# Keeping split weights in DRAM for later chunks

## The chip, the core and the metric

One Trainium2 chip, of which the kernel uses one core. The metric is the device time of one execution in microseconds (us). [...]

## The reference

One layer of a decoder with four kinds of token mixers side by side, over 2048 tokens of width 1024, and an MLP of width 4096 behind them. The shapes that matter here: w_in has 1024 rows and 3852 columns, w_out is 1024 x 1024.

```python
h = _modulate(x, norm_mix_gain[l], shift1, scale1)
z = (h @ w_in[l]).astype(jnp.float32)
(hq, hf, hi, hg, dq, dk, dv, fq, fk, fv, fg, ff, mq, mk, mv, mo, mi, mf) = _split(z, IN_WIDTHS)
y_a = _hgrn2(hq, hf, hi, hg, ...)            # gated linear recurrence
y_b = _diff_attention(dq, dk, dv, ...)       # two score maps, mixed
y_c = _forgetting_attention(fq, fk, fv, fg, ff, ...)
y_d = _mlstm(mq, mk, mv, mo, mi, mf, ...)    # matrix memory recurrence
y = jnp.concatenate([y_a, y_b, y_c, y_d], axis=-1) @ w_out[l]
x = x + (gate1[:, None, :] * y).astype(x.dtype)
h = _modulate(x, norm_ff_gain[l], shift2, scale2)
y = jnp.square(jax.nn.relu(h @ w_ff1[l])) @ w_ff2[l]
x = x + (gate2[:, None, :] * y).astype(x.dtype)
```

## The kernel before

The tokens are worked in four chunks of 512. The mixing part is written as two strands whose steps are woven into each other. Strand a is attention: for each chunk the forgetting attention (fox_attn), then the differential attention (diff_attn). Strand b first makes queries, keys and values of all four chunks (seven loads of weights a chunk), and then, chunk by chunk, the dense products and the serial parts of the two recurrences (mlstm, hgrn), each in two halves; as soon as attention has finished a chunk, the output projection of that chunk follows (w_out_dense), and then the second norm. After the mixing part comes the MLP.

The order of the instructions on each engine is not the written one: a scheduler plans it before the run, from priorities and from a simulation of its own. Each engine, and the queue of SP, from which almost all DMAs are issued, then works its list in that order: one that waits holds all that stand behind it.

Weights come in by load_w (L199). It takes the next of two tiles for the high part (whi, 128 x 8 x 268) and the next of two for the low part (wlo). The 1024 rows of a load go in pieces through four raw buffers: for 256 columns four pieces of 256 rows. For a piece, SP issues the DMA of the raw weights (L208; two DMAs where the columns come from two places, as in win2, L948), ACT rounds it into the high part (L194), and POOL subtracts the high part from the raw piece, which gives the low part (L197). So a raw buffer is free again when POOL is done with it, and a weight tile when the last matmul that reads it is done. A load is used by dense_cm (L509 to L511, 24 matmuls for 128 output columns with all 512 tokens) or by dense_tm (L521 to L523, 24 matmuls for 128 tokens), once for all tokens of the chunk.

A chunk's recurrences make nine loads: four for mlstm (L1003, L1016, for both halves), and for hgrn two with two pieces of columns (L1130), two of 128 columns (L1138) and one of 256 (L1145). Its output projection makes four (L1307). The same weights are loaded and split again for each of the four chunks.

What else the prediction names: L679 are the score matmuls, L686 is DVE's eviction of scores with a running minimum, L695 is ACT's exponential, L881 is DVE's mixing of the two score maps of the differential attention, L734 are the transposes behind it, L737 (ACT) and L738 (DVE) split a transposed map into its parts, L748 are the products with the values. L647 and L660 load keys, queries and values for attention from DRAM. L1211 to L1215 are levels of hgrn. L243 and L249 are ada: the modulation vector is made block by block on DVE from w_ada; 16 of its blocks, each with four loads of 256 KB through two buffers, are spread over the serial parts of the recurrences of the first two chunks.

Of the kernel before, what the change touches and what calls it, by code (L numbers as in the profile page):

```python
# [9 lines left out]
F32 = mybir.dt.float32  # L10
# [60 lines left out]
def hybrid_block(ctx: ExitStack, tc: tile.TileContext, a: dict, out: bass.AP, dbg: dict):  # L71
# [124 lines left out]
            nc.vector.tensor_copy(h, r)  # L196
        nc.gpsimd.tensor_tensor(l, r, f32(h), ALU.subtract)  # L197

    def load_w(pieces, n, stage=raws):  # L199

        h, l = ring(whi), ring(wlo)
        step = stage[0].shape[1] // n
        for k0 in range(0, KT, step):
            ks = slice(k0, k0 + step)
            r = ring(stage)[:, :step * n].rearrange("p (k n) -> p k n", k=step)
            for c0, src in pieces:
                w = src.shape[-1]
                nc.sync.dma_start(r[:, :, c0:c0 + w], src[k0 * P:(k0 + step) * P].rearrange("(k p) n -> p k n", p=P))  # L208
            split_w(r, h[:, ks, :n], l[:, ks, :n])
        return h, l  # L210

    w_in = a["w_in"][0]
# [263 lines left out]
    if True:  # L476
# [469 lines left out]
            return pc  # L946

        def win2(c0, c1):  # L948
            return load_w([(0, w_in[:, c0:c0 + P]), (P, w_in[:, c1:c1 + P])], G)


        gates_of = {}
# [176 lines left out]
        def hgrn_dense(c, j, st):  # L1129
            W = win2(O_HF + j * P, O_HQ + j * P)  # L1130
            st["fq"] = []
            for blk in range(2):
                o = dense_cm(W, blk)
                st["fq"].append(FB.get())
                with soon("b"):
                    nc.scalar.activation(FB[st["fq"][blk]][:, :CT], o, AF.Copy)
                yield
            o = dense_cm(win(O_HG + j * P, P), 0)  # L1138
            st["g"] = FB.get()
            with soon("b"):  # L1140
                nc.vector.tensor_copy(FB[st["g"]][:, :CT], o)
            yield

            if j == 0:
                W = win(O_HI)  # L1145
                hval[c] = (FB.get(), FB.get())
                for tb in range(TB):
                    o = dense_tm(W, tb, G)
                    with soon("b"):
                        nc.scalar.activation(tok(hval[c][0], P)[:, tb], o[:, :P], AF.Copy)  # L1150
                        nc.vector.tensor_copy(tok(hval[c][1], P)[:, tb], o[:, P:G])
                    yield
# [134 lines left out]
        def w_out_dense(c, st, u):  # L1287
# [16 lines left out]
                t0 = c * CT + tb * P  # L1304
                nc.sync.dma_start(FB[xs[tb]][:, :512], a["x"][0, t0:t0 + P, u * 512:(u + 1) * 512])
            for n in range(2):
                W = load_w([(0, a["w_out"][0][:, u * 512 + n * G:u * 512 + (n + 1) * G])], G)  # L1307
                ns = slice(n * G, (n + 1) * G)
                for tb in range(TB):
                    o = dense_tm(W, tb, G, st["h"])  # L1310
# [506 lines left out]
```

## Time and profile before

| | us |
|---|---|
| median of 3 runs | 3220.86 |
| lowest, highest | 3217.7, 3223.13 |
| the profiled execution | 3222.74 |
| its span, first to last instruction | 3221.0 |
| busy in the span: TensorE, DVE, ACT, POOL | 2973.0, 2053.9, 1650.5, 777.6 |
| granted clock, mean | 0.945 |

Times in the rows below are counted from the start of the span of the profiled execution. A group of instructions is given by its line in the kernel, its engine, its operation and the names of what it writes and reads, with the number of instructions behind the x. Busy time of an engine is the union of its instructions; matmuls are pipelined, so a busy TensorE is not TensorE at its peak. The granted clock is the share of full speed that TensorE had.

### The profile page before, as it was taken

The numbers are of one execution on the slowest core, as the hardware profiler recorded it, in microseconds if no ns is written. First come the engines' busy times: TensorE is split into PE (matmuls) and PEld (weight loads), VectorE is DVE, ScalarE is ACT, GpSimd is POOL, SyncE is SP. The second block draws the span as 40 slices with busy tenths as digits, with TensorE's granted clock in tenths as the row PEclk, the third lists the DMA queues.
The fourth block names the chain that finished last, engine by engine and source line by source line (L and its number), as shares of the span: only waits on it lengthen the run. The fifth ranks groups of instructions, "written<-read, shape, count | busy, mean of one in ns | idle before, by whom it ended". The sixth has DMA issues, their size and how long they took to land.

```text
span 3221.0 us, 50522 instructions
## 1 busy us (share of the span) xinstructions
PE 2973.0 (92%) x17398; PEld 2494.0 (77%) x17398; DVE 2053.9 (64%) x4642; ACT 1650.5 (51%) x3576; POOL 777.6 (24%) x800
## 2 busy tenths in 40 slices
PE   5989999899888899999988679999999999999999
PEld 3878989678667688887777467888788778887887
DVE  4377567767768867766778638666866545445553
ACT  2566667556545556556555536555555533332331
POOL 3454344334334344444344120000000000000000
PEclk8999999889889799999989789999999999999999
DMA  6876766535434364545343345555555577566662
GB/s 230 267 238 213 243 219 206 186 113 172 125 105 149 117 199 116 163 135 173 92 144 117 100 150 169 152 149 155 172 157 152 167 235 238 183 194 214 222 205 76
DMA packets 506565, 548.70 MB, mean 170 GB/s; under 512 B 41401, under 2 KB 352788, under 8 KB 504260
## 3 DMA queue, kind: packets, MB, share of 16 engines
q1 hardware_dynamic: 504004, 541.28, 53.4%
q10 hardware_dynamic: 2304, 4.20, 0.4%
q8 instruction: 137, 2.24, 0.3%
q14 instruction: 120, 0.98, 0.1%
HBM read 385.83 MB, written 159.51 MB: 169 GB/s over the span
## 4 chain that ended last, share of the span: by engine, by line
PE 53%; DVE 13%; DMA 6%; ACT 3%; issue 2%; POOL 1%; SPq 0%; DVEq 0%; POOLq 0%; ACTq 0%
PE bank L1560 6%; PE bank L1561 6%; PE bank L1559 5%; PE bank L1782 5%; PE bank L1781 5%; PE bank L1780 5%; PE bank L142 3%; PE bank L521 2%; PE bank L748 2%; PE bank L523 2%; PE bank L522 2%; PE bank L679 2%; PE bank L734 2%; DMA stage<-in_w_ff 2%; DVE FA L881 2%
## 5 line engine op out<-in xcount | busy, mean ns | idle before, releaser
L197 POOL TENSOR_TENSOR wlo<-raw,whi 128x512 fp32r<-128x512 f32 (+1 forms) x304 | 408.7, 1364 | 387.1 <-ACT whi L194 346.0
L521 PE MATMUL bank<-whi,AH 128*128 128x256 f32 (+1 forms) x1536 | 452.3, 295 | 25.1 <-ACT whi L194 11.1
L522 PE MATMUL bank<-wlo,AH 128*128 128x256 f32 (+1 forms) x1536 | 445.7, 290 | 0.9 <-POOL wlo L197 0.9
L523 PE MATMUL bank<-whi,AH 128*128 128x256 f32 (+1 forms) x1536 | 444.8, 290 | 0.0
L695 ACT ACTIVATE FA<-FA,att_m 128x512 f32<-128x512 f32 (+3 forms) x480 | 310.5, 650 | 153.4 <-DVE att_m L692 146.2
L686 DVE TENSOR_SCALAR_CACHE_REDUCE FA<-bank 128x512 f32<-128x512 f32 (+3 forms) x480 | 284.3, 603 | 69.6 <-PE bank L679 40.0
L521 PEld LDWEIGHTS bank<-whi,AH 128*128 128x128 f32 x1536 | 299.1, 195 | 35.9 <-ACT whi L194 11.4
L522 PEld LDWEIGHTS bank<-wlo,AH 128*128 128x128 f32 x1536 | 299.4, 195 | 3.8 <-POOL wlo L197 1.4
L523 PEld LDWEIGHTS bank<-whi,AH 128*128 128x128 f32 x1536 | 298.4, 195 | 2.7 <-issue 1.9
L679 PE MATMUL bank<-AL 97*128 97x512 f32 (+10 forms) x640 | 241.9, 436 | 57.1 <-DVE FA L686 53.8
L748 PE MATMUL bank<-TS,AL 128*128 128x256 f32 (+1 forms) x1152 | 238.4, 314 | 15.7 <-DVE TS L738 7.2
L194 ACT ACTIVATE whi<-raw 128x512 fp32r<-128x512 f32 (+1 forms) x304 | 186.5, 628 | 114.9 <-PE bank L523 45.0
L737 ACT ACTIVATE TS<-bank 128x512 fp32r<-128x512 f32 (+1 forms) x288 | 158.8, 569 | 135.0 <-PE bank L734 118.5
L738 DVE TENSOR_TENSOR TS<-bank,TS 128x512 fp32r<-128x512 f32 (+1 forms) x288 | 185.7, 654 | 63.3 <-ACT TS L737 60.2
L734 PE MATMUL bank<-ident,FA 128*128 128x128 f32 x1088 | 198.9, 292 | 24.9 <-DVE FA L881 24.0
L748 PEld LDWEIGHTS bank<-TS,AL 128*128 128x128 f32 x1152 | 186.5, 203 | 35.8 <-DVE TS L738 11.6
L679 PEld LDWEIGHTS bank<-AL 97*128 97x128 f32 (+2 forms) x640 | 122.1, 208 | 94.5 <-DVE FA L686 78.6
L734 PEld LDWEIGHTS bank<-ident,FA 128*128 128x128 f32 x1088 | 139.7, 150 | 38.5 <-DVE FA L881 28.5
L509 PE MATMUL bank<-AH,whi 128*128 128x512 f32 x384 | 159.1, 419 | 7.1 <-DVE FB L1107 2.1
L510 PE MATMUL bank<-AH,whi 128*128 128x512 f32 x384 | 159.0, 414 | 2.5 <-DMA AH<-hl 2.5
L511 PE MATMUL bank<-AH,wlo 128*128 128x512 f32 x384 | 157.9, 411 | 0.0
L881 DVE SCALAR_TENSOR_TENSOR FA<-FA,att_ro,FA 128x512 f32<-128x512 f32 (+3 forms) x160 | 128.2, 848 | 1.2
(908 smaller groups left out, 7478.2 us busy)
## 6 DMA issues: line engine op xcount, KB each, us to landing
r<-tmp SPq DMA_DIRECT2D x224, 256.0 KB
raw<-in_w_in SPq DMA_DIRECT2D x144, 256.0 KB
stage<-r SPq DMA_DIRECT2D x139, 256.0 KB
stage<-in_w_ff SPq DMA_DIRECT2D x32, 1024.0 KB
stage<-in_w_ff SPq DMA_DIRECT2D x107, 256.0 KB
raw<-in_w_in SPq DMA_DIRECT2D x192, 128.0 KB
tmp<-r SPq DMA_DIRECT2D x85, 256.0 KB
AL<-kD SPq DMA_DIRECT2D x80, 224.0 KB
```

The lines of the kernel that those rows point to most:

```text
L197: nc.gpsimd.tensor_tensor(l, r, f32(h), ALU.subtract)
L521: nc.tensor.matmul(o[:, :n], hTh[:, k, t], h[:, k, :n], start=(k == 0), stop=False)
L522: nc.tensor.matmul(o[:, :n], hTh[:, k, t], l[:, k, :n], start=False, stop=False)
L523: nc.tensor.matmul(o[:, :n], hTl[:, k, t], h[:, k, :n], start=False, stop=(k == KT - 1))
L679: nc.tensor.matmul(o[:, :w], lh, rh(p)[:, :w], start=(i == 0), stop=(i == len(mm) - 1 and not diag))
L686: nc.vector.tensor_scalar(FA[e][:, :w], o[:, :w], -1.0, 3.0e38, ALU.mult, ALU.min, accum_out=st[:, p:p + 1])
L695: nc.scalar.activation(FA[e][:, :w], FA[e][:, :w], AF.Exp, scale=-1.0, bias=mx, accum_out=sz[:, p:p + 1] if n > 1 else z)
L734: nc.tensor.transpose(o[:, c0:c0 + P], FA[e][:, (sb % 4) * P:(sb % 4 + 1) * P], ident)
L748: nc.tensor.matmul(*mms[n], start=(m == 0 and i == 0), stop=(last and i == 3))
L881: nc.vector.scalar_tensor_tensor(x0, x1, ro, x0, ALU.mult, ALU.add)
L1560: nc.tensor.matmul(o, h, xl, start=False, stop=False, skip_group_check=True)
L1561: nc.tensor.matmul(o, l, xh, start=False, stop=last, skip_group_check=True)
```

## The change

load_w gets a key. When it is called with a key for the first time, it loads and splits as before, and then stores both parts, as they lie in whi and wlo, into two DRAM tiles of their own (two DMAs, a whole part each). When it is called with a key that it knows, it takes the next pair of weight tiles and issues four DMAs from those DRAM tiles into them, the high and the low part of the first half of the rows, then of the second half: no raw buffer, no instruction on ACT or POOL. The thirteen loads of the recurrences and of the output projection get keys; those of attention's queries, keys, values and gate get none.

```diff
+    split_d = {}
+
+    def load_w(pieces, n, stage=raws, key=None):
         h, l = ring(whi), ring(wlo)
+        if key in split_d:
+            for ks in (slice(0, KT // 2), slice(KT // 2, KT)):
+                for t, d in zip((h, l), split_d[key]):
+                    nc.sync.dma_start(f32(t[:, ks, :n]), d[:, ks])
+            return h, l
         step = stage[0].shape[1] // n
...
             split_w(r, h[:, ks, :n], l[:, ks, :n])
+        if key is not None:
+            split_d[key] = [dr.tile([P, KT, n], F32, name=nm("wsplit")) for q in "hl"]
+            for t, d in zip((h, l), split_d[key]):
+                nc.sync.dma_start(d, f32(t[:, :, :n]))
         return h, l
...
         def win2(c0, c1):
-            return load_w([(0, w_in[:, c0:c0 + P]), (P, w_in[:, c1:c1 + P])], G)
+            return load_w([(0, w_in[:, c0:c0 + P]), (P, w_in[:, c1:c1 + P])], G, key=c0)
...
-            o = dense_cm(win(O_HG + j * P, P), 0)
+            o = dense_cm(load_w([(0, w_in[:, O_HG + j * P:O_HG + (j + 1) * P])], P, key=O_HG + j * P), 0)
...
-                W = win(O_HI)
+                W = load_w([(0, w_in[:, O_HI:O_HI + G])], G, key=O_HI)
...
-                W = load_w([(0, a["w_out"][0][:, u * 512 + n * G:u * 512 + (n + 1) * G])], G)
+                W = load_w([(0, a["w_out"][0][:, u * 512 + n * G:u * 512 + (n + 1) * G])], G, key=-1 - 2 * u - n)
```

## Rows read from the trace of the kernel before

**Rows 1.** By stage: length, busy PE, PEld, DVE, ACT, POOL; clock, DMA share, GB/s
```profile
560.00:780.00 220.00, 203.62 (x1278) 168.02 (x1278) 162.16 (x447) 120.65 (x286) 86.27 (x86) 0.89 0.49 152
780.00:1160.00 380.00, 326.09 (x2236) 271.95 (x2231) 295.89 (x784) 198.54 (x471) 140.47 (x152) 0.87 0.42 127
1160.00:1453.00 293.00, 287.90 (x2168) 251.02 (x2167) 200.98 (x511) 182.14 (x418) 133.97 (x142) 0.98 0.50 157
1453.00:1784.00 331.00, 297.06 (x2111) 254.45 (x2110) 244.08 (x643) 192.98 (x457) 141.21 (x145) 0.93 0.43 135
1784.00:1905.00 121.00, 89.83 (x578) 76.26 (x576) 55.35 (x135) 53.98 (x125) 28.27 (x29) 0.82 0.32 103
```
**Rows 2.** TensorE's groups, 780 to 1905: busy, mean ns | idle before, its releasers
```profile
L521 PE MATMUL bank<-whi,AH 128*128 128x256 f32 x672 | 200.2, 298 | 10.8 <-DVE FB L1236 6.3 <-ACT FB L1085 1.4 <-ACT FB L1232 1.2
...
L679 PE MATMUL bank<-AL 97*128 97x512 f32 (+8 forms) x382 | 152.4, 456 | 48.3 <-DVE FA L686 47.2
L734 PE MATMUL bank<-ident,FA 128*128 128x128 f32 x716 | 129.4, 297 | 16.5 <-DVE FA L881 15.8 <-DVE TS L738 0.4
```
**Rows 3.** The chain: shares by line, 780 to 1905; pieces from 560 on (start, length)
```profile
by line: PE bank L142 7.6%; PE bank L521 6.4%; PE bank L523 6.1%; PE bank L522 6.0%; PE bank L748 6.0%; PE bank L679 5.2%; PE bank L734 4.8%; DVE FA L881 4.5%; ACT FA L695 4.3%; DVE FA L686 4.1%; issue 3.9%; PE bank L509 3.8%; PE bank L510 
...
777.36 2.54 POOL wlo L197 x2
...
1630.33 1.44 POOL wlo L197
```
**Rows 4.** The two instructions of a split, 780 to 1905, on POOL and ACT
```profile
L197 POOL TENSOR_TENSOR wlo<-raw,whi 128x512 fp32r<-128x512 f32 x152 | 206.4, 1374 | 134.8 <-ACT whi L194 107.0 <-DMA raw<-in_w_in 16.2 <-PE bank L679 7.7
...
L194 ACT ACTIVATE whi<-raw 128x512 fp32r<-128x512 f32 x152 | 93.0, 627 | 65.3 <-PE bank L523 36.7 <-PE bank L510 27.1
```
**Rows 5.** DVE's groups by shape, 780 to 1905, with three lines' min/median/max ns
```profile
L686 DVE TENSOR_SCALAR_CACHE_REDUCE FA<-bank 128x512 f32<-128x512 f32 x240 | 161.9, 684 | 36.2 <-PE bank L679 26.9 <-PE bank L734 7.5 <-PE bank L682 0.7
L738 DVE TENSOR_TENSOR TS<-bank,TS 128x512 fp32r<-128x512 f32 x158 | 106.2, 684 | 43.5 <-ACT TS L737 43.1
L881 DVE SCALAR_TENSOR_TENSOR FA<-FA,att_ro,FA 128x512 f32<-128x512 f32 x88 | 79.5, 954 | 0.7
...
L249 DVE SCALAR_TENSOR_TENSOR ST<-FB,cact,ST 128x256 f32<-128x256 f32 x35 | 23.2, 662 | 9.5 <-DMA FB<-in_w_ada 9.2
L1214 DVE TENSOR_TENSOR FB<-FB,FB 128x256 f32<-128x256 f32 x39 | 20.7, 530 | 3.8 <-ACT FB L1213 3.7
...
L1215 DVE TENSOR_TENSOR FB<-FB,FB 128x256 f32<-128x256 f32 x31 | 18.5, 596 | 0.0
...
L249 DVE SCALAR_TENSOR_TENSOR ST<-FB,cact,ST x35: 469/485/1501, 817.4 to 1126.3; 128x256 f32<-128x256 f32 x35
L1214 DVE TENSOR_TENSOR FB<-FB,FB x39: 405/425/1514, 781.7 to 1735.8; 128x256 f32<-128x256 f32 x39
L1215 DVE TENSOR_TENSOR FB<-FB,FB x31: 396/419/1512, 782.1 to 1736.1; 128x256 f32<-128x256 f32 x31
```
**Rows 6.** DVE's groups by shape, 1800 to 1850, where POOL is idle
```profile
L686 DVE TENSOR_SCALAR_CACHE_REDUCE FA<-bank 128x512 f32<-128x512 f32 x10 | 6.8, 686 | 1.8 <-PE bank L679 1.0 <-PE bank L682 0.7
L881 DVE SCALAR_TENSOR_TENSOR FA<-FA,att_ro,FA 128x512 f32<-128x512 f32 x7 | 4.8, 748 | 0.0
```
**Rows 7.** The page's DMA queue: packets, MB, share of 16 engines' span
```profile
q1 hardware_dynamic: 504004, 541.28, 53.4%
```
**Rows 8.** L249's idle time by releaser (560 to 1160); SP's wait (780 to 1905)
```profile
  DMA FB<-in_w_ada: 18.6, 13
  DMA ST<-in_w_ada: 2.3, 2
...
SPq L208 <- POOL wlo L197: 166.8, 86, 15.0
```
**Rows 9.** L521 alone, two stretches: length, busy PE, PEld; clock, DMA share, GB/s
```profile
1867.30:1880.40 13.10, 9.30 (x33) 6.08 (x33) 1.00 0.67 219
1880.40:1891.90 11.50, 9.17 (x33) 6.17 (x33) 1.00 0.45 141
```

More of the change, by code (lines that the diff above doesn't have):

```diff
@@ L197, in split_w @@
         nc.gpsimd.tensor_tensor(l, r, f32(h), ALU.subtract)
-    def load_w(pieces, n, stage=raws):
+    split_d = {}
+    def load_w(pieces, n, stage=raws, key=None):
         h, l = ring(whi), ring(wlo)
+        if key in split_d:
[3 more added lines that the diff above has]
+            return h, l
         step = stage[0].shape[1] // n
```

## The prediction

> **What bounds the kernel now.** I read the table by stage first [rows 1]. The change touches the weights of the recurrences and of the output projection, and these run in the four stages from 560 to 1905 us; before them come the attention projections, which keep their splits, and after them the MLP, which calls load_w nowhere. In 780 to 1905, where later chunks reuse weights, TensorE is busy for 1000.9 of 1125 us: it idles 53.9 + 5.1 + 33.9 + 31.2 = 124.1 us. That is the first ceiling of any gain, apart from the granted clock, which is 0.87 where most of that idle time lies (780 to 1160) and 0.98 where there is nearly none (1160 to 1453).
>
> Second, what TensorE waits for there [rows 2]. The reader should look for the splits and not find them: the first matmul on fresh weights (L521, 672 of them) idles 10.8 us, and DVE and ACT lines of the recurrences end most of it. No wait on L194 or L197 is among the three that end most. The long waits are for DVE: 47.2 us for the score eviction L686, and 15.8 us for the mixing of two score maps, L881. So the splits do not starve TensorE directly; if they cost time, they cost it through DVE, or by standing in line on ACT and POOL.
>
> Third, the chain that ended last over the same stretch [rows 3]: L881 has 4.5% of it (50.6 us), L695 4.3%, L686 4.1%. L197 has no share among the lines shown, but shows up in five pieces of over 1 us, at 777, 1399, 1401, 1627 and 1630 us, of which the first and the last stand there.
>
> **What is removed.** A chunk's recurrences split 32 pieces and its output projection 16, so 48 in each of three later chunks, 144 of 304 on each engine. At 627 ns and 1374 ns [rows 4] that is 90 us of ACT and 198 us of POOL. In 780 to 1905 there are 152 of them, of which the 16 of the first chunk's output projection stay; the other 8 removed ones lie just before 780. Most of this is beside other work, and four things reach the path.
>
> (a) L197 on the chain: the five pieces are 2.54, 1.27, 1.25, 1.43 and 1.44 us, 7.9 us in all, each a split of a later chunk. Removed, 7.9 us.
>
> (b) DVE beside L197. L881 takes 954 ns in 780 to 1905 [rows 5] and 748 ns in 1800 to 1850, where POOL does nothing [rows 6]: 88 x 206 = 18.1 us. L249 takes 662 ns against a median of 485: 35 x 177 = 6.2 us. L1214: 39 x (530 - 425) = 4.1 us; L1215: 31 x (596 - 419) = 5.5 us. Together 33.9 us. All four read two tensors in SBUF. L686 (240 of them, 684 ns here and 686 ns in the stretch without POOL) reads PSUM and pays nothing. L197 is 206.4 of POOL's 443.9 busy us in these stages [rows 1, 4], so its part lies between 46% of the 33.9 us and all of it; I take three quarters, because the long POOL instructions are the ones that can hold a DVE instruction for long, and scale by 136 of 152: 23 us of DVE. L881 has 50.6 us on the chain of the 79.5 us that its main form is busy and about 92 with its short forms, so 55%: 12.6 us.
>
> [...]
>
> (c) ACT's line. L194 holds ACT for 93.0 us and idles it for 65.3 us more, waiting for the last matmul that reads the old weights [rows 4]; L695 and L737 stand behind it. DVE waits for L737 for 43.1 us in L738's main form [rows 5]. L194 occupies 158 of 1125 us, 14%; that share of 43.1 is 6 us. The chain shows nothing of it, so it lies between 0 and 6: I take 3.
>
> (d) The clock. If (a) to (c) take a fifth of the 124 us of idle time, the 326 us of matmul at 0.87 may move a fifth of the way to 0.93 (the level of 1453 to 1784): all of it would be 326 x (1 - 0.87/0.93) = 21 us, a fifth 4 us. Bounds 0 and 21.
>
> Sum of gains: 7.9 + 12.6 + 3 + 4 = 27.5 us.
>
> **What is added.** In the first chunk each of 13 loads gets two stores, of 25 MB in all (9 loads in the recurrences, 16.8 MB, and 4 in the projection, 8.4 MB). In later chunks a load moves 2.1 MB instead of 1.05: 3 x 12.6 = 38 MB more. Together 63 MB. The queue moved 541 MB in 53.4% of the span [rows 7], so 315 GB/s when busy: 63 MB are 200 us of the DMA engines, over a stretch of 1345 us in which they are busy 0.32 to 0.50 [rows 1]. That is hidden on average; a full load takes 6.7 us where it took 3.3. Issues fall: 72 per later chunk become 52, and 26 stores come once.
>
> (e) Who is queued with it: the loads of w_ada (L243), on the same SP queue, until 1160. DVE's L249 waits 20.9 us for them [rows 8]. In 560 to 1160 come the 25 MB of stores and 8.4 MB of doubled loads, 107 us of DMA in 600 us, so a share of 0.45 becomes 0.63: waits scaled by 1.4 are 8 us more, half of them on the path: 4 us. Bounds 0 and the rival's price below.
>
> (f) The load now lands in the weight tile itself and so can only be issued when the last matmul on that tile is done; before, the raw piece came early and only the split waited. The cover is the time of the other tile's matmuls. It is shortest at the end, where nothing else runs: 32 or so L521 take 13.1 and 11.5 us [rows 9], in which DMA is already busy 0.67 and 0.45, 8.8 and 5.2 us. With 3.3 us more that makes 12.1 and 8.5: it just lands. 2 us, bounds 0 and 6. Elsewhere attention's matmuls stretch the cover.
>
> (g) The new wait stands on SP, for TensorE. SP waits today at the same place, 166.8 us in 86 waits, for L197 to free a raw piece [rows 8]; behind it stand attention's keys and values (L647, L660), the residual (L1305) and L243. The new wait ends when a tile comes free, some splits earlier than the old one ended. I take 0, and 10 to either side.
>
> (h) Every engine's order is planned anew by the scheduler from its own simulated times. No row prices that. The same planner left 5.1 us idle of 293 in one stage and 53.9 of 380 in another [rows 1], 2% and 14%; a sixth of that difference over 1125 us is 22 us, to either side. I take 0.
>
> Net: -27.5 + 4 + 2 = -21.5 us. From the profiled execution's 3222.74 us (span 3221.0) that is 3201; the median of the three runs is 1.9 us below the profiled one, so I forecast **3200 us**.
>
> **The rivals.**
> *No change (3221).* The gains are off the path: DVE's shorter L881 only brings forward the wait for L686 or L695, which are next on the chain [rows 3] and as long as before, and (a) goes into the POOL instructions behind. For it: L686 holds TensorE three times as long as L881 does. Against it: L881 has the largest share on the chain of any line that is not TensorE's. That a key never matches, so that nothing is loaded back, ends here too; each load has its own column as key, and I give it almost nothing.
> *Slower, through the queue.* Stores and doubled loads stand ahead of w_ada's 64 loads (16 blocks of four) on SP in 560 to 1160, and DVE, in order, stops at L249 with L686 behind it, for which TensorE waits. If half of the 64 loads come one half load (3.3 us) later, DVE stops for 106 us; with half of that on the path, 53 us: 3201 - 4 + 53 = 3250. It decides from about a quarter of that effect, 26 us of DVE stops more than today's 20.9, at which it eats the net gain. For it: DVE stops for these loads 15 times already [rows 8]. Against it: the DMA engines are half idle there.
> *Much faster (3175).* All of (b) belongs to L197 and the clock takes its whole 21 us: 7.9 + 17 + 6 + 21 - 6 = 46 us.
>
> **How the numbers follow.** Chances: forecast 0.53 (3181 to 3214), much faster 0.07, no change 0.18, slower 0.22. Below 3170 and above 3236 I leave about 2 in 10, so the range is 3170 to 3236; it takes in (d), (g) and (h) and the first half of the slower rival. About 0.2%, 6.4 us, can be told from no change; faster by more than that 0.60, within 0.18, slower 0.22. Since both signs have weight: the forecast's own range is 3181 to 3214.
>
> **What the profile of the changed kernel would show.** L194 and L197 with 160 instructions each instead of 304. L881 near 800 ns in the same stretch ((b) right), or still above 900 (wrong: other POOL work holds it). Matmuls L521 and L509 without a wait for DMA of weights ((f) right). L249's waits for w_ada below 30 us ((e) right), or above 47 (the slower rival). DMA bytes near 612 MB. Were the gain there and L881 unchanged, the cause would be ACT's line or the plan; were L881 short and the time the same, the first rival holds. The forecast is wrong if TensorE waits for weights in more than the last two loads, or if the new plan idles TensorE more than (h) allows.

## The result and the profile after

The changed kernel takes **3180.43 us** (median of four executions, 3177.96 to 3183.32), the kernel before 3219.28 us on the same chip: a ratio of 0.9869, 95% interval 0.9849 to 0.9888. The gain is 39 us, where the prediction's step gave 21. The profiled execution took 3180.53 us with a span of 3178.8, at a granted clock of 0.947 (before: 3222.74, 3221.0, 0.945).

The first lines of the page of after, its main queue, and its transfers of whole halves of split weights:

```profile
PE 2951.4 (93%) x17398; PEld 2481.0 (78%) x17398; DVE 2010.9 (63%) x4642; ACT 1571.3 (49%) x3432; POOL 586.1 (18%) x656
...
DMA packets 554145, 611.58 MB, mean 192 GB/s; under 512 B 40857, under 2 KB 400372, under 8 KB 551844
...
q1 hardware_dynamic: 551588, 604.19, 59.6%
...
whi<-wsplit SPq DMA_DIRECT2D x66, 512.0 KB
```

The queue's 604 MB stand against 541 in [rows 7]: 63 MB more, as worked out. Lines after the edit stand 12 lower in after: L521 is L533, L679 is L691, L686 is L698, L734 is L746, L881 is L893, L249 is L261.

**Where the time went.** I cut each execution at three events that all kernels have: the last matmul of the attention projections, the last dense product of the first chunk's recurrences (the serial part of its hgrn goes on behind it, to 881 us in before), and the last matmul of the output projection. Columns are as in [rows 1]. The two stretches between them, for before (two executions, the second from e16), after (two, the second from e9), and e17, which is told below, in this order:

```profile
564.00:775.50 211.50, 195.12 (x1186) 160.38 (x1185) 154.89 (x430) 114.81 (x270) 79.92 (x81) 0.89 0.49 148
775.50:1903.20 1127.70, 1005.37 (x7142) 857.49 (x7140) 800.00 (x2077) 629.74 (x1474) 447.71 (x470) 0.91 0.44 136
```
```profile
572.10:779.80 207.70, 193.58 (x1185) 158.53 (x1184) 155.10 (x430) 114.74 (x270) 79.06 (x81) 0.89 0.50 150
...
779.80:1901.50 1121.70, 998.69 (x7141) 851.27 (x7139) 794.81 (x2077) 630.08 (x1474) 447.48 (x470) 0.92 0.44 136
```
```profile
575.70:766.10 190.40, 179.22 (x1187) 150.08 (x1186) 150.19 (x424) 108.89 (x259) 73.97 (x76) 0.97 0.78 251
766.10:1868.40 1102.30, 989.73 (x7140) 846.98 (x7138) 759.00 (x2087) 556.40 (x1340) 262.13 (x330) 0.91 0.56 180
```
```profile
569.20:759.70 190.50, 179.94 (x1188) 150.63 (x1186) 149.41 (x425) 108.90 (x259) 74.12 (x76) 0.96 0.78 250
...
759.70:1865.70 1106.00, 994.55 (x7140) 851.78 (x7138) 760.77 (x2087) 556.94 (x1340) 262.42 (x330) 0.91 0.56 179
```
```profile
570.90:778.70 207.80, 191.74 (x1221) 159.03 (x1220) 156.35 (x437) 111.31 (x267) 73.15 (x76) 0.93 0.52 162
778.70:1873.00 1094.30, 988.08 (x7105) 844.52 (x7104) 754.62 (x2073) 555.86 (x1333) 262.91 (x330) 0.92 0.54 173
```

The reader should see two gains of the same size. In the long stretch, where weights are reused, the mean of two executions goes from 1124.7 to 1104.2 us: **-20.5 us**. In the first chunk's recurrences (short for the stretch up to the second cut), where 16.8 MB of stores are added and next to nothing is removed (four subtractions and six roundings of the second chunk's loads, in its last 40 us), it goes from 209.6 to 190.5 us: **-19.2 us**. The rest is the attention projections (568.1 to 572.5, with every engine's instructions in the same order in both kernels up to 545 us, and 8.1 and 6.5 us between the two executions of one kernel, so this is scatter) and the MLP with what else stands behind the mixing (1317.8 to 1311.7; no run says why). Together -41.4 us, the difference of the mean spans.

The long stretch falls apart further. The same 7140 matmuls are busy for 1002.0 us before and 992.1 after (-9.9), and TensorE idles 122.7 and 112.0 us (-10.6). Adding the view of TensorE's waits up by the engine that ended them, DVE ended 100.2 us before and 77.7 after (-22.5), DMA 11.1 and 22.5 (+11.4), ACT 7.1 and 6.4, POOL 1.7 and 2.4. The -9.9 cannot be called the clock's: the granted clock of the stretch is 0.91 and 0.92 before, 0.91 and 0.91 after, and two executions of the same kernel differ by 6.7 and 4.8 us in this sum.

After's groups on TensorE and on DVE there, and two of SP's waits (total, times, longest), which answer to [rows 2, 5, 8], columns as there:

```profile
L533 PE MATMUL bank<-whi,AH 128*128 128x256 f32 x672 | 198.2, 295 | 14.3 <-DVE FB L1248 6.7 <-ACT FB L1097 2.6 <-DVE ST L1210 1.5
...
L691 PE MATMUL bank<-AL 97*128 97x512 f32 (+9 forms) x390 | 151.7, 445 | 42.2 <-DVE FA L698 27.7 <-DMA AL<-kD 8.7 <-DMA AH<-yl 3.2
L746 PE MATMUL bank<-ident,FA 128*128 128x128 f32 x716 | 127.8, 295 | 15.7 <-DVE FA L893 15.4 <-DVE TS L750 0.2
```
```profile
L698 DVE TENSOR_SCALAR_CACHE_REDUCE FA<-bank 128x512 f32<-128x512 f32 x242 | 163.4, 685 | 47.6 <-PE bank L691 36.3 <-PE bank L746 6.1 <-PE bank L694 3.8
L750 DVE TENSOR_TENSOR TS<-bank,TS 128x512 fp32r<-128x512 f32 x158 | 106.6, 684 | 34.1 <-ACT TS L749 33.7
L893 DVE SCALAR_TENSOR_TENSOR FA<-FA,att_ro,FA 128x512 f32<-128x512 f32 x88 | 65.9, 799 | 0.7
...
L261 DVE SCALAR_TENSOR_TENSOR ST<-FB,cact,ST 128x256 f32<-128x256 f32 x35 | 21.4, 611 | 5.3 <-DMA FB<-in_w_ada 4.9
```
```profile
SPq L208 <- PE bank L535: 76.1, 27, 16.9
SPq L208 <- PE bank L523: 54.6, 20, 10.9
```

L893 takes 799 ns where it took 954; L698, which reads PSUM, takes 685 where it took 684. TensorE's wait for the score eviction falls from 47.2 to 27.7 us though the eviction itself is as long: DVE reaches it sooner. New in these rows is DMA, at the score matmuls: attention's keys (kD) 8.7 us (5.9 in e9), and yl, the low part of the mixers' output on its way to the projection, 3.2 us. The longest of the waits for DMA beside them is not new, that for yh, the high part; before, then after:

```profile
PE bank L521 <- DMA AL<-yh: 8.1, 3, 6.9
```
```profile
PE bank L533 <- DMA AL<-yh: 7.8, 2, 7.0
```

SP's two waits in the group above (L208 is in after the load from the new DRAM tiles) are the new wait for a free weight tile: 130.7 us, where the wait for L197 was 166.8.

### The profile page after: what moved, and what is told of

Its sections match the earlier page's. It is cut to its first block, busy times and chain, and to the rows that moved or that the text cites. A ratio compares the mean times of both kernels' runs of the same rounds, so it can differ in the third digit from the quotient of the medians.

```text
span 3178.8 us, 49931 instructions
## 1 busy us (share of the span) xinstructions
PE 2951.4 (93%) x17398; PEld 2481.0 (78%) x17398; DVE 2010.9 (63%) x4642; ACT 1571.3 (49%) x3432; POOL 586.1 (18%) x656
## 2 busy tenths in 40 slices
DMA packets 554145, 611.58 MB, mean 192 GB/s; under 512 B 40857, under 2 KB 400372, under 8 KB 551844
## 4 chain that ended last, share of the span: by engine, by line
PE 69%; DVE 14%; DMA 9%; ACT 4%; issue 2%; SPq 1%; POOL 0%; ACTq 0%; DVEq 0%; POOLq 0%
PE bank L1572 6%; PE bank L1573 6%; PE bank L1794 6%; PE bank L1793 6%; PE bank L1571 6%; PE bank L1792 5%; PE bank L533 5%; PE bank L535 5%; PE bank L534 5%; PE bank L760 3%; PE bank L142 3%; PE bank L691 3%; PE bank L746 3%; PE bank L521 2%; PE bank L522 2%; DVE FA L698 2%
## 5 line engine op out<-in xcount | busy, mean ns | idle before, releaser
L533 PE MATMUL bank<-whi,AH 128*128 128x256 f32 (+1 forms) x1536 | 451.5, 295 | 27.0 <-ACT whi L194 11.1
L698 DVE TENSOR_SCALAR_CACHE_REDUCE FA<-bank 128x512 f32<-128x512 f32 (+3 forms) x480 | 284.7, 603 | 78.4 <-PE bank L691 45.8
L533 PEld LDWEIGHTS bank<-whi,AH 128*128 128x128 f32 x1536 | 298.0, 194 | 37.4 <-ACT whi L194 12.3
L691 PE MATMUL bank<-AL 97*128 97x512 f32 (+11 forms) x640 | 236.6, 427 | 49.5 <-DVE FA L698 33.6
L197 POOL TENSOR_TENSOR wlo<-raw,whi 128x512 fp32r<-128x512 f32 (+1 forms) x160 | 216.2, 1372 | 271.9 <-ACT whi L194 231.0
L746 PE MATMUL bank<-ident,FA 128*128 128x128 f32 x1088 | 196.0, 291 | 18.3 <-DVE FA L893 17.8
L691 PEld LDWEIGHTS bank<-AL 97*128 97x128 f32 (+2 forms) x640 | 119.2, 204 | 82.0 <-DVE FA L698 57.1
L746 PEld LDWEIGHTS bank<-ident,FA 128*128 128x128 f32 x1088 | 138.5, 149 | 29.6 <-DVE FA L893 22.2
L521 PE MATMUL bank<-AH,whi 128*128 128x512 f32 x384 | 155.0, 408 | 5.9 <-DVE FB L1119 3.1
L522 PE MATMUL bank<-AH,whi 128*128 128x512 f32 x384 | 155.2, 404 | 0.5 <-DMA AH<-hl 0.5
L194 ACT ACTIVATE whi<-raw 128x512 fp32r<-128x512 f32 (+1 forms) x160 | 98.7, 629 | 48.7 <-DMA raw<-in_w_in 25.4
L893 DVE SCALAR_TENSOR_TENSOR FA<-FA,att_ro,FA 128x512 f32<-128x512 f32 (+3 forms) x160 | 117.0, 779 | 1.2
```

Of the source, the lines that this page charges most:

```text
L521: nc.tensor.matmul(o, wh, hTh[:, k, :], start=(k == 0), stop=False)
L522: nc.tensor.matmul(o, wh, hTl[:, k, :], start=False, stop=False)
L533: nc.tensor.matmul(o[:, :n], hTh[:, k, t], h[:, k, :n], start=(k == 0), stop=False)
L691: nc.tensor.matmul(o[:, :w], lh, rh(p)[:, :w], start=(i == 0), stop=(i == len(mm) - 1 and not diag))
L698: nc.vector.tensor_scalar(FA[e][:, :w], o[:, :w], -1.0, 3.0e38, ALU.mult, ALU.min, accum_out=st[:, p:p + 1])
L746: nc.tensor.transpose(o[:, c0:c0 + P], FA[e][:, (sb % 4) * P:(sb % 4 + 1) * P], ident)
```

## The experiments

My theory: POOL's subtraction slows DVE's instructions with two SBUF inputs (L881 took 954 ns in the mean of 780 to 1905 and 748 where POOL was idle [rows 5, 6]), and DVE holds TensorE (47.2 us of waits for L686 [rows 2]). The rivals were ACT's line, the queue's cost, and the new plan. The ratio stands to the kernel before, with its 95% interval; the changed kernel is 0.9869. Diffs are against the changed kernel except for e5.

**POOL or ACT?** e3 loads the low part and the raw weights, so only POOL's subtraction goes; e2 loads the high part and the raw weights, so only ACT's rounding goes. Both load as many bytes as after and store half.

```
# e3                                   # e2
-for t, d in zip((h, l), split_d[key]):
-    nc.sync.dma_start(...)
+nc.sync.dma_start(f32(l[:, ks, :n]), got[:, ks])     # e2: h
...
+nc.scalar.activation(h[:, ks, :n], r, AF.Copy)       # e2: gpsimd.tensor_tensor(l, r, h)
```

> Later chunks load the low part from DRAM and the raw weights too; ACT rounds as before the change, POOL subtracts nothing. WORK with POOL as its carrier: L881 near 800 ns, the time 3183 to 3195, close to the changed kernel. If ACT's line were the carrier: 3205 to 3220. PLAN: anything from 3190 to 3215.

> Later chunks load the high part from DRAM and the raw weights too; POOL subtracts as before the change, ACT rounds nothing. Bytes moved in later chunks as in the changed kernel, stores half. WORK with POOL as its carrier: L881 stays near 950 ns and the time at 3208 to 3220 (ACT's share is at most 6 us by the prediction's step c). If ACT's line were the carrier: 3185 to 3195. PLAN: anything from 3190 to 3215, not ordered by which engine is relieved.

e3: 3199.52 us, 0.9911 [0.9882, 0.9939]. e2: 3232.9 us, 1.0028 [1.0003, 1.0052]. At equal bytes loaded and stored, leaving out the subtraction is worth 1.17% more than leaving out the rounding, 38 us (33 us between the two medians). Both times lie above what WORK, my theory, had put on record for them; e3's is one that PLAN allowed. DVE's mixing in the two, e3 first:

```profile
L894 DVE SCALAR_TENSOR_TENSOR FA<-FA,att_ro,FA 128x512 f32<-128x512 f32 x88 | 65.6, 798 | 1.0
```
```profile
L894 DVE SCALAR_TENSOR_TENSOR FA<-FA,att_ro,FA 128x512 f32<-128x512 f32 x88 | 79.0, 948 | 0.6
```

Both stand as theory wants: 798 ns without the subtraction, 948 with it. This mean moves with the order too: it is 875 ns in e1, which subtracts everywhere (e1 is told below). e3's long stretch is 1100.0 us, as short as after's, and e2's 1153.5; their first chunk's recurrences are 209.0 us, as in before, and 192.9, nearly as in after. So taking ACT's rounding away as well gave nothing in the long stretch.

e5 is the kernel before with the subtraction left out of the later loads, and no store or load added:

```
-            split_w(r, h[:, ks, :n], l[:, ks, :n])
+            if key in split_d:
+                nc.scalar.activation(h[:, ks, :n], r, AF.Copy)
+            else:
+                split_w(r, h[:, ks, :n], l[:, ks, :n])
```

> The kernel before, in which later chunks of the keyed loads leave out POOL's subtraction (the low part of the weights is then not computed there): no stores, no loads from DRAM, raw weights and ACT's rounding as before. It has the relief of POOL without the added DMA. From the end of the first chunk's recurrences to the end of the mixing part the kernel before takes 1128 us, the changed one 1102, the one with POOL's work put back 1154. If the relief is worth 52 us there and the added DMA costs 26 (the difference that the run with POOL's work back shows against the kernel before), this stretch takes about 1076 and the whole 3160 to 3180. If the DMA is hidden and the relief worth 26, it takes 1095 to 1105 and the whole 3185 to 3200.

3197.56 us, 0.9907 [0.9874, 0.9939], as e3: POOL's work alone is worth some 0.9% of the 1.3%. The time lies in the second of the two forecasts; the long stretch, in the profiled execution, which at 3211.51 us is the slowest of the four, misses both:

```profile
783.20:1892.50 1109.30, 1000.93 (x7142) 853.29 (x7140) 752.98 (x2077) 628.86 (x1473) 258.15 (x330) 0.91 0.44 138
```

DVE is busy for 753.0 us where before has 797.4, DVE ends 83.1 us of TensorE's waits where it ended 100.2, and the mixing takes 837 ns. No load, no store and no rounding differ from before here.

e4 puts the subtraction back into the changed kernel, into a buffer that nothing reads:

```
         if key in split_d:
...
+                nc.gpsimd.tensor_tensor(r, r, f32(h[:, ks, :n]), ALU.subtract)
             return h, l
```

> The changed kernel, with one POOL instruction of the removed kind and size (it reads a raw buffer and the loaded high part, writes the raw buffer; nobody reads the result) put back for each of the 144 removed. Nothing on the path waits for them, but POOL is as busy as before and DVE meets them. WORK through DVE: L881 back at 920 to 960 ns and the time at 3195 to 3210, half to three quarters of the gain lost. If POOL only cost by the split being late: 3180 to 3186. PLAN: 3170 to 3195, in no relation to L881.

3232.13 us, 1.0014 [0.9994, 1.0033]: the whole gain is gone, 1.45% or 47 us, more than was put on record for any theory. Nobody waits for the result. Its groups for the mixing on DVE and for the score matmuls on TensorE, in 766 to 1915:

```profile
L898 DVE SCALAR_TENSOR_TENSOR FA<-FA,att_ro,FA 128x512 f32<-128x512 f32 x88 | 72.7, 878 | 0.6
```
```profile
L696 PE MATMUL bank<-AL 97*128 97x512 f32 (+10 forms) x385 | 155.2, 462 | 64.7 <-DVE FA L703 61.9 <-DMA AL<-kD 2.1
```

TensorE waits 61.9 us for the score eviction where it waited 27.7; the eviction itself takes 684 ns as ever. The place is the queue on DVE ahead of it. But DVE's lengthening is not all: DVE is busy for 796 us in e4's long stretch, as long as in before (797), and the stretch is 29 us longer than before's. There is a second carrier. The added subtraction reads the loaded weights, so POOL stands still until they land, with the recurrences' POOL work behind it; the idle time of POOL before it (us, times), and then the long stretch:

```profile
  DMA whi<-wsplit: 199.6, 63
```
```profile
761.00:1915.00 1154.00, 1011.85 (x7137) 861.97 (x7136) 796.24 (x2082) 560.16 (x1340) 447.83 (x470) 0.90 0.54 172
```

ACT's waits for POOL in that stretch come to 113 us, where they are 61 in before and 74 in after; in e2, whose subtraction reads a loaded part as well, they are 112. e4's 47 us are the price of both carriers.

The long stretches of the runs so far (and of e1), in us:

| | later loads as before | later loads from DRAM, or half of them and the raw weights |
|---|---|---|
| POOL subtracts | 1127.7, 1121.7 (before), 1128.6 (e1) | 1153.5 (e2), 1154.1 (e4) |
| POOL does not | 1109.3 (e5) | 1102.3, 1106.0 (after), 1100.0 (e3) |

ACT rounds in before, e1, e3 and e5 and not in the others. Without the added loads the relief is worth some 15 us in the profiled executions (25 by e5's median), beside them some 50: where POOL subtracts, the loads cost 29 us, and where it does not, nothing that stands out. Orders alone move this stretch by 10 us: e14, the changed kernel with its stores on another queue (told below), has 1095.5.

e6 and e7 were to say whether POOL must read SBUF for that. For each split removed e6 has two memsets, e7 one subtraction of tiles that are there anyway:

```
+                nc.gpsimd.memset(r, 0.0)                                            # e6, twice
+                nc.gpsimd.tensor_tensor(r, r, raws[0][:, :step * n], ALU.subtract)  # e7
```

> The changed kernel with two POOL memsets of a raw buffer for each of the 144 removed subtractions: POOL is occupied but reads nothing from SBUF and waits for nothing but itself. PORT (DVE instructions with two SBUF inputs are held while POOL reads): no harm, L881 within 20 ns of the changed kernel's 799 and 3178 to 3190. LINE (other POOL work stands behind the added instructions): 3200 to 3230, in proportion to the time that POOL is occupied.

> The changed kernel with one POOL subtraction of two raw buffers for each of the 144 removed: the same operation and size as in the run with POOL's work put back, but it does not wait for the loaded weights. PORT: as there, 3215 to 3235, with L881 at 860 to 960 ns. If the harm there came from POOL standing still for the load with the recurrences' work behind it: 3180 to 3195, whatever L881 takes.

e6: 3213.43 us, 0.9968 [0.9951, 0.9985], where PORT allowed 3190 at most and LINE began at 3200. e7: 3223.74 us, 1.0013 [0.9992, 1.0034], as PORT had it, though its mixing takes 829 ns for a forecast of 860 and more. Both are hard to read, since nothing orders the added work and the planner put most of it into the third of five stages, from the end of the first chunk's output projection to that of the second's: in e6 187 memsets between 1151 and 1483, in e7 POOL busy for 191.7 us between 1161 and 1489 against 68.1 in after. That stage grew to 331.2 and 328.1 us from 295.4, while the one after it, with none of the added work, took 296.9 and 291.2 (after: 287.1 and 289.2). So POOL's work costs time in the stage in which it runs. e7 waits for no load, ACT's waits for POOL are 72.7 us in its long stretch, as in after, and DVE is busy for 794.7 us; it costs as much as e4. So the harm does not need POOL standing still. In e6 the mixing takes 808 ns, near after's, and nearly all of the harm is two long holds of DVE, which the last section shows. Whether e7's harm comes through longer DVE instructions alone is not settled. PORT is a theory's name: the runs show how long DVE's instructions take beside POOL's work, and no run shows a port.

**What does the queue cost?** e8 adds the old raw loads, read by nobody: 38 MB. e10 loads the high part alone, with the same three matmuls for each product (high x high, high x low, low x high): half the bytes and half the issues.

```
+                    nc.sync.dma_start(r[:, :, c0:c0 + w], src[...])          # e8
-                for t, d in zip((h, l), split_d[key]):
-                    nc.sync.dma_start(f32(t[:, ks, :n]), d[:, ks])
+                nc.sync.dma_start(f32(h[:, ks, :n]), split_d[key][0][:, ks]) # e10
```

> The changed kernel that also loads the raw weights in later chunks, into the raw buffers, where nobody reads them: 38 MB more on the same queue and 72 issues more a chunk, nothing else. If added DMA costs the path what the difference of 26 us suggests for a like number of bytes: 3195 to 3215. If it is hidden, as the prediction had it: 3178 to 3188.

> The changed kernel, in which later chunks load only the high part from DRAM; the low part is left as the tile last held it (so the products with it are not those of the weights, though as many). It has the relief of ACT and POOL with half of the loads' DMA, 1.05 MB a load as before the change. If the added DMA of the changed kernel costs the path some 10 to 26 us: 3155 to 3172. If it is hidden: 3176 to 3186.

e8: 3220.02 us, 0.9990 [0.9974, 1.0006], 38 us more than after and above both forecasts. e10: 3164.4 us, 0.9823 [0.9802, 0.9844], 16 us less, and its long stretch is 1088.7 us against 1102.3 and 1106.0. The score matmuls of e8, and then of e10:

```profile
L697 PE MATMUL bank<-AL 97*128 97x512 f32 (+9 forms) x390 | 155.1, 455 | 53.5 <-DVE FA L704 34.1 <-DMA AL<-kA 13.8 <-DMA AL<-kD 4.3
```
```profile
L690 PE MATMUL bank<-AL 97*128 97x512 f32 (+10 forms) x390 | 154.3, 453 | 29.9 <-DVE FA L697 27.1 <-DMA AL<-kA 1.5 <-DMA AL<-kD 0.5
```

What the transfers hold up here are attention's keys: 18.1 us in e8, 8.7 in after, 2.0 in e10. All of TensorE's waits that DMA ended come to 34.5, 22.5 and 13.1 us in the long stretch. Yet the order counts as much as the bytes: with as many bytes loaded as in after they are 13.5 in e3, 13.4 in e4 and 11.1 in e14, as in before (11.1), and e13, below, has a long stretch of 1087.0 us with all of after's bytes. So e10's 16 us are not shown to be the price of the bytes. e8 also spreads raw buffers and issues over SP, so its 38 us are not a price of bytes alone.

e13 makes rows longer, not fewer bytes: both tiles are viewed without the unused half of each row, so a 256-column load is one contiguous piece per partition. e12 issues the loads from POOL, e14 the stores from ACT.

```
-        h, l = ring(whi), ring(wlo)
+        h, l = (ring(w).rearrange("p k n -> p (k n)")[:, :KT * n].rearrange("p (k n) -> p k n", n=n) for w in (whi, wlo))   # e13
-                    nc.sync.dma_start(f32(t[:, ks, :n]), d[:, ks])
+                    nc.gpsimd.dma_start(f32(t[:, ks, :n]), d[:, ks])         # e12
-                nc.sync.dma_start(d, f32(t[:, :, :n]))
+                nc.scalar.dma_start(d, f32(t[:, :, :n]))                     # e14
```

> The changed kernel with the weight tiles used without gaps between the rows of 256 columns, so that a stored or loaded part is one run of 4 to 8 KB a partition instead of runs of 1 KB (512 B where a part has 128 columns). The bytes are the same. If the added DMA costs the path some 17 us by the time its packets take: 3165 to 3176, with the DMA share lower at the same GB/s. If only bytes count: 3178 to 3186. The order of the instructions changes from the first loads on, which may move it by 10 us to either side.

> The changed kernel with the loads from the new DRAM tiles issued from POOL's queue instead of SP's; the wait for a weight tile then stands on POOL, with the recurrences' POOL work behind it, and SP's line (loads of keys, values, w_ada) is free of it. If the new wait on SP is what costs (prediction's step g): 3160 to 3176. If it is harmless there, and harmful on POOL: 3190 to 3225.

> The changed kernel with the first chunk's stores issued from ACT's queue instead of SP's: the same work, another order from the first chunk's recurrences on. If the 21 us gained there belong to the order of the changed kernel, its stretch from the end of the attention projections to the end of the first chunk's recurrences moves to anywhere between 190 and 211, and the whole by as much, 3180 to 3200. If they came from the stores leaving SP's line or from anything in the work, it stays at 190 to 195.

e13: **3171.11 us**, 0.9844 [0.9820, 0.9868], with 470945 packets for 554145. It is the fastest kernel here that does all the work; its interval and the changed kernel's overlap, so only its lead over before is shown. e12: 3202.88 us, 0.9929 [0.9899, 0.9959], 20 us worse than after or so. Two things changed on POOL, and the run does not part them: it waits for tiles, and the issues themselves keep it busy, 114.7 us for 150 of them in 762 to 1871:

```profile
L208 POOL DMA_DIRECT2D wlo<-wsplit x75 | 57.4, 765 | 38.9 <-PE bank L535 33.3 <-PE bank L534 1.9 <-PE bank L523 1.3
L208 POOL DMA_DIRECT2D whi<-wsplit x75 | 57.3, 764 | 111.4 <-PE bank L523 98.5 <-DVE att_zc L710 9.5 <-PE bank L691 1.3
```

e14: 3187.73 us, 0.9901 [0.9876, 0.9925], nothing gained; its first chunk's recurrences take 197.6 us, between the two kernels' as the order was expected to have it.

**Where do the first chunk's 19 us come from?** e1 has the stores and no load from them; e9 and e16 are the changed kernel and the one before, unaltered; e17 has after's later loads with two stores in place of 26.

```
-        if key in split_d:
-            ...
-            return h, l
-        if key is not None:
+        if key is not None and key not in split_d:   # e1
...
+            if n == G and None not in split_d:       # e17: one pair is stored, all later loads read it
+                split_d[None] = ...
+            split_d[key] = split_d[None]
```

> The stores alone: the first chunk's thirteen loads are stored in DRAM (25 MB), later chunks load and split the raw weights as before the change. Two theories. WORK: the 40 us come from the removed POOL and ACT work (DVE freed of POOL, POOL and ACT lines shorter); then this run has no gain and pays for the stores: 3219 to 3227. PLAN: a good part comes from the new order of instructions, which already differs in the first chunk's recurrences, where nothing is removed (that stretch became 21 us shorter in the profile after); then this run, whose order there is that of the changed kernel, is at 3195 to 3208, and ends its first recurrences some 20 us earlier than before, relative to the end of the attention projections.

> The changed kernel once more, unaltered, on the chip of the other runs of this set. Two questions: how far single stretches move from one profiled execution to the next with the very same instructions (the attention projections, 0 to about 570, have the same order in every kernel so far and took 564 to 576; the first chunk's recurrences took 190 to 211), and whether the 1.3% holds. If the gain is the removed work and the order: ratio 0.984 to 0.990. If the 3180 were a lucky chip: 0.990 to 0.998. A stretch that differs by 10 us from the first profile of this kernel could not be explained by work or order.

> The kernel before, unaltered, for a second profile. If the order fixes the stretch of the first chunk's recurrences, it takes 207 to 214 us again (211.5 in the first profile), and the stretch from there to the end of the mixing part 1120 to 1135 (1127.7). If single profiles scatter by 10 us and more, the readings by stretch fall.

> After with two stores in place of 26: only the first load of 256 columns is stored, and every later keyed load reads those two tiles again, so as many bytes and packets are loaded as in after but the weights of the later loads are another column's. It tells apart whether the first chunk's recurrences (190 us in both profiles of after, 208 to 212 in those of before) are shorter because of the stores or only because everything was planned anew, and what 23 MB of stores cost. Theory (the planner's new order, of which the stores are one cause among others): the stretch lies anywhere between 190 and 212 us, and the total follows it: 3170 to 3195 us. Rival (the stores' own DMA costs time on the path): the first stretch stays near 190 us and the total falls by 5 us or more below 3180, as the half load did. Second rival (the stores make that order, and without them the first chunk runs as in before): the stretch is again near 208 us or more and the total near 3195 to 3200 us.

e1: 3217.17 us, 0.9970 [0.9951, 0.9989]. e9: 3181.03 us, 0.9873 [0.9856, 0.9890]. e16: 3220.91 us. e17: 3195.87 us, 0.9914 [0.9885, 0.9944]. The repeats show that 190 and 208 to 212 us belong to the kernels and are not scatter. e1 lies between its two theories: with the stores alone the order is not yet the changed kernel's. In e17, as its second rival had it, the first chunk's stretch is back at 207.8 us and the time 15 us above after's (the intervals just touch), while its long stretch is 1094.3 us, 10 us shorter than after's; there DMA ends 13.3 us of TensorE's waits where it ended 22.5. Of these differences some 5 us each way are work that moved across the cut: e17 has 34 matmuls more than after in the first stretch and 35 fewer in the long one. The 5 us that are left in the long stretch are within what orders move, so a price of the stores there is not shown. e1 has the stores too, and 204.8 us: here neither the stores without the later loads nor the later loads without most of the stores gave the short stretch. And e2 and e3, which store equally many bytes there, take 192.9 and 209.0 us: it is not the bytes but the order that differs.

What differs in that stretch can be read. Columns as in [rows 1], steps of 20 us that start at the same event, the end of the attention projections plus 40 us; before, then after:

```profile
604.00:624.00 20.00, 15.64 (x62) 11.61 (x62) 15.14 (x48) 10.20 (x25) 9.24 (x9) 0.83 0.42 116
624.00:644.00 20.00, 14.72 (x99) 11.27 (x97) 19.83 (x79) 9.12 (x26) 4.53 (x4) 0.81 0.41 130
644.00:664.00 20.00, 19.83 (x96) 14.58 (x97) 13.74 (x41) 8.61 (x23) 0.30 (x1) 0.76 0.21 66
```
```profile
616.00:636.00 20.00, 18.96 (x111) 15.67 (x110) 16.55 (x60) 12.53 (x28) 9.67 (x7) 1.00 1.00 320
636.00:656.00 20.00, 17.74 (x109) 14.02 (x107) 18.21 (x66) 10.59 (x33) 3.32 (x3) 0.83 0.66 213
656.00:676.00 20.00, 18.21 (x129) 13.24 (x127) 17.62 (x39) 10.35 (x22) 6.95 (x7) 1.00 0.52 154
```

In before DVE is full for 20 us (19.83) and TensorE has work for 15.64 and 14.72 of 20; the granted clock of the steps falls to 0.76, and 257 matmuls get done in 60 us. In after TensorE has work for 18.96 and 17.74 of 20, the clock is 1.00 again in the third step, and 349 get done. The repeats, e16 and e9, have 0.83, 0.73, 0.76 and 1.00, 0.74, 1.00 in the same steps. Over the stretch 1187 matmuls are busy for 179.2 us at a clock of 0.97 where 1186 took 195.1 at 0.89 (the fences that cut the executions), and 195.1 x 0.89 and 179.2 x 0.97 are both 174 us: by that, 16 of the 21 us between these two executions are the clock, 15 of the 19 between the means. That the order of the first chunk's work lets TensorE idle less there is shown; why the planner chose it is not.

**How far should it reach?** e15 keeps only the recurrences' weights, e11 the attention projections' as well.

```
-                W = load_w([(0, a["w_out"][0][...])], G, key=-1 - 2 * u - n)
+                W = load_w([(0, a["w_out"][0][...])], G)                      # e15
-            return load_w([(0, w_in[:, c0:c0 + n])], n)
+            return load_w([(0, w_in[:, c0:c0 + n])], n, key=c0)               # e11
```

> The changed kernel with keys for the recurrences alone; the output projection loads and splits as before the change. Two thirds of the removed splits (96 of 144). If relief goes by the number of splits: two thirds of the gain, about 3194. If the output projection's loads, of which the last eight stand at the end of the mixing part with nothing else to hide them, cost more than their splits did: 3180 or less.

> The changed kernel with keys for the seven loads of attention's queries, keys, values and gate too, so that 80 more of the 160 splits are gone, at 15 MB of stores and 22 MB of loads more in 0 to 570, where the DMA engines are busy 0.71 already and DVE only 0.6. If relief of POOL is worth the same there: 3160 to 3175. If DVE is not what that stretch waits for and DMA is: 3185 to 3210, with waits for DMA at the first matmul of a load.

e15: 3196.91 us, 0.9925 [0.9895, 0.9956], a little over half of the gain with two thirds of the splits; most of it is its first chunk's recurrences (193.4 us), its long stretch is 1117.6. e11: 3221.21 us, 0.9997 [0.9980, 1.0013]: all of the gain is lost, which neither forecast had. Its attention projections take 581.5 us, in a band of 564 to 577 for the others; the rest is spread over later stages (206.6 us in the first chunk's recurrences, 137.9 in the last projection against 129.6). The cause was not taken further.

## Where the prediction failed, and what held

The gain was 39 us for a forecast of 21. **The long stretch came out as the sum said:** -20.5 us against -21.5. Its terms did so partly by making up for each other, which is luck:

| step | forecast | measured in the long stretch |
|---|---|---|
| (a) + (b), TensorE held by DVE and by L197 | -20.5 | -22.5 of waits that DVE ended; POOL ended 1.7 before and 2.4 after, so (a) cannot be seen by itself |
| (c) ACT's line | -3 | -0.7 of waits that ACT ended; e3 against after gives nothing |
| (d) clock | -4 | -9.9 of busy time of the same matmuls, at a granted clock of 0.91 to 0.92 in both |
| (e) + (f), transfers | +6 | +11.4 of waits that DMA ended; none in e14, with the same bytes in another order |
| (g) SP's new wait | 0 | 130.7 us of wait for 166.8; what it costs was not measured |

**(h), the new plan, is the step that failed.** It was put at nothing, with 22 us to either side; the plan gave 19 us in the first chunk's recurrences, a stretch that the prediction did not cost beyond its stores. 15 of these 19 us are TensorE's clock, which (d) had looked for in the long stretch alone. That the bound held is luck: it was worked out over the 1125 us of the long stretch, and the same 2% of the first chunk's 211 us would be 4 us. Why the planner's order is the better one stays open.

**(b) was right in DVE's relief and in L881's time,** 799 ns for a forecast near 800; e2, which subtracts, has 948 ns and e3, which does not, 798. The four lines gave 88 x 155 + 35 x 51 + 39 x 19 + 31 x 98 ns = 19.2 us (L1214 and L1215 now take 511 and 498 ns) against 23; but DVE as a whole is 37.5 us shorter in the long stretch (797.4 to 759.9), so as much came free in lines that were not in the sum. TensorE's waits for DVE fell by 22.5, in which (a), (c) and the new order have their part as well. L686, which (b) left out since it took 684 ns in that stretch and 686 where POOL was idle, stayed as it was: 685 ns, 163.4 us.

**(e) named the wrong customer.** L261's waits for w_ada in 566 to 1160 come to 20.8 us, below the bound of 30, as before's 20.9; two of them, from the view of DVE's waits in after:

```profile
DVE FB L261 <- DMA FB<-in_w_ada: 8.4, 5, 4.0
...
DVE FB L261 <- DMA ST<-in_w_ada: 7.5, 5, 2.1
```

The new waits stood at attention's keys (8.7 us) and at yl (3.2 us) instead, which are on the same queue; by the table of long stretches the loads would have cost 29 us had POOL gone on subtracting, a tie between the relief and the loads that the sum did not have. (f) itself held: TensorE waits for a load from wsplit in one place, 0.8 us, and once, 2.1 us, behind a store.

**The rivals.** No change fell with e5: without POOL's later subtractions, and with loads, stores and rounding as before, DVE is 44 us shorter, TensorE waits 17 us less for it, and the time is 0.9% less, so POOL's work is on the path. Slower through the queue did not come, as L261 shows; but e8 shows that it was near: 38 MB more and the gain is gone. Much faster gave a time near the measured one (3175) by another way, 46 us in the long stretch, which gave 20.5.

**The other signs** were as put: 160 splits on POOL and ACT, and 611.58 MB.

## What to carry to other kernels

Work on POOL that nobody waits for can still hold TensorE, by lengthening DVE's instructions ahead of the one that TensorE needs (in e4 the mixing took 878 ns for 799, and TensorE waited 61.9 us for the score eviction instead of 27.7), and by standing ahead of POOL's own work (ACT waited 113 us for POOL instead of 74): look at the DVE group's mean time with and without POOL beside it, and count all of DVE's lines, not only the largest. Keeping a result in DRAM to save that work paid here; price the added transfers at the loads behind them on their queue and at the engine that has to wait for them, for the same loads cost 29 us beside POOL's subtractions and nothing that stood out without them. Longer rows (e13) gave the fastest kernel, 3171.11 us, but its lead over after is not shown. Where a planner orders every engine anew, a stretch that the edit doesn't touch can move by as much as the edit itself; compare each stretch with its own repeat before any cause is given.

## What the runs showed of the hardware

In e6 two small DVE instructions each lasted until the end of a whole run of POOL's memsets, not of one of them. The timeline, with start and length in us, and TensorE's two waits behind them (total, times, longest):

```profile
1155.54 26.68 POOL L213 MEMSET raw<- 128x512 f32 x57
...
1156.72 25.52 DVE L279 TENSOR_SCALAR nw_ms<-pss 128x4 f32<-128x4 f32 x1
...
1158.41 23.84 DVE L703 TENSOR_SCALAR_CACHE_REDUCE FA<-bank 128x512 f32<-128x512 f32 x1
```
```profile
PE bank L696 <- DVE FA L703: 20.1, 1, 20.1
PE bank L142 <- DVE FB L1041: 17.7, 1, 17.7
```

A TENSOR_SCALAR of 128x4, whose median is 170 ns over its eight instructions of that shape, took 25.52 us, and it ends with the last of 57 memsets of some 0.47 us that stand back to back. The score eviction behind it, 685 ns elsewhere, is drawn at 23.84 us. A COPY of 64x4 at 1234.95 took 19.61 us and ends with the last of 40 packed memsets; two other packed runs, of 20 and 29, held no DVE instruction for 2 us. Behind the two holds TensorE waits 37.8 us, and e6's third stage is 36 us longer than after's. Why these two were held for a whole run of memsets, no run shows. POOL's work may be cheaper for DVE with gaps in it than packed; no run here tried that.
